# ScalarE multiplies and shifts x itself in a transformer layer's prologue, and first-feature products and transposes are reordered

## The chip, the cores and the metric

The kernel runs on one core of a Trainium2 chip. A core has five engines with instruction queues of their own: TensorE (PE in the profile; its weight loads are PEld) for matrix products and transposes, VectorE (DVE), ScalarE (ACT), GpSimd (POOL), and SyncE (SP), which here issues the transfers from DRAM. Operands lie in SBUF, products collect in PSUM. Semaphores order the engines among each other, and every engine works off its own queue in order.

The metric is the device time of one execution in microseconds, compared by the median over runs.

## The reference

One layer of a diffusion backbone works on 128 context tokens and 512 latent tokens, 1024 features wide. Only its first steps matter here: a normalisation, a modulation by conditioning vectors (one pair of scale and shift per feature for the context tokens, another for the latent tokens), and the product with the input weights, of which the prologue takes the key and value columns.

```python
ada_ctx = (jax.nn.silu(c_ctx) @ w_ada[i] + b_ada[i])[None, None, :]
ada_lat = (jax.nn.silu(c) @ w_ada[i] + b_ada[i])[:, None, :]
...
sh1, sc1, g1, sh2, sc2, g2 = jnp.split(ada, N_ADA, axis=-1)
u = rms_norm(h, p["g_pre1"]) * (1 + sc1) + sh1
z = u @ p["w_in"]
q, k, v, b_gate, c_gate, x_in, g_att, g_conv = jnp.split(z, idx, axis=-1)
```

Behind that stand attention, a gated convolution, the output projections and a convolutional feed-forward part. They make up most of the time, and the change does not touch them.

## The kernel before

Inputs are float32. A float32 product is made of three products of split operands: each operand is divided into a high part, rounded to the type `fp32r`, and a low part, the remainder. `mm3` (lines 182 to 185) adds high by high (L183), high by low weights (L184) and low by high weights (L185). The roundings are ScalarE copies, the remainders VectorE subtractions.

The 640 tokens are five tiles of 128 (tile 0 is context), the 1024 features eight blocks of 128, called features below: the first is number 0. The prologue goes so:

- The five token tiles are loaded into `XT`, squared on ScalarE (L351), normalised on VectorE into `xn` (L356), transposed by TensorE (`x_turn`, L361: eight 128x128 transposes for one tile) into PSUM, and copied to `xT` with features on the partitions (`x_copy`, L367 on ScalarE and L369 on VectorE).
- For each feature scale and shift are computed from `w_ada`. The features go in groups: (0), (1), (2, 3), (4, 5), (6), (7). `ada1_mm(g, i)` (L379) multiplies the conditioning vectors with the group's columns, i = 0 for scale and 1 for shift; each call is eight matmuls. `ada1_copy` (L386) brings the sums to SBUF as `e`, by ScalarE. `ada1_fold` (L393) sums partial results by a product with `sel`, and two VectorE instructions for each feature (L396, L398) write its columns of `scsh`: scale and shift for latent and context tokens. `ada1_fold(2, (0,))` does feature 2, `ada1_fold(2, (1,))` feature 3 alone.
- `modulate(f, a, b)` (L403 to L416) makes the operand of feature f for tokens a to b. VectorE writes `u`, x times scale plus shift, in one instruction for context tokens and one for latent tokens (L411). ScalarE rounds it into the high part `UH` (L413). VectorE subtracts for the low part `UL` (L416).
- `fetch` and `cut_upto` load the weight units of `w_in` (`raw`) and split them, `whi` by ScalarE (L148) and `wlo` by VectorE (L149); the first unit is split by lines of its own (L476, L478).
- `kv_mm(f, ts)` (L418) adds feature f's three products for the token tiles ts into the PSUM sums of keys and values, all 512 columns at once.

The order of TensorE, ScalarE and VectorE is written out by hand, and each runs its instructions in just the order of the code; SyncE's too in the prologue. What is written first is first in the queue, and an instruction that waits holds up all behind it on its engine. The lines around the first three features:

```python
        ada1_mm(1, 0)
        kv_mm(0, (0, 1))
        modulate(0, 512, NTOK)
        cut_upto(2)
        ada1_mm(1, 1)
        ...
        kv_mm(0, (2,))
        ada1_fold(1)
        kv_mm(0, (3, 4))
        modulate(1, 0, 384)
        modulate(1, 384, NTOK)
        ada1_mm(2, 0)
        ada1_copy(2, 0, 1)
        kv_mm(1, (0, 1))
```

From feature 2 on a loop does the same for each feature: ada products where a group is due, the split of the next unit, `kv_mm` for tiles 0 and 1, fold and `modulate` of the next feature, `kv_mm` for tiles 2 to 4.

`XT` is used again: once normalised, its rows take columns of `w_ada` for later groups. The region of `xT` for features 4 to 7 is used again as `AR`, for a later stage's columns of `w_ada`, loaded at L229 and used at L235.

Of the kernel before, what the change touches and what calls it, by code (L numbers as in the profile page):

```python
# [13 lines left out]
AF = mybir.ActivationFunctionType  # L14
ALU = mybir.AluOpType
# [3 lines left out]
KT = 8  # L19
# [44 lines left out]
def trunk_layer(ctx, tc, x_prompt, x_sample, cache_k, cache_v, c, c_ctx, w_ada, b_ada, g_pre1, g_post1, g_pre2,  # L64
# [3 lines left out]
    V, S, G, PE = nc.vector, nc.scalar, nc.gpsimd, nc.tensor  # L68
# [25 lines left out]
    def nm(s):  # L94
        cnt[0] += 1
        return f"{s}_{cnt[0]}"

    def region(pool, tag, shape, dtype, name):
        return pool.tile([128] + shape, dtype, tag=tag, name=name)
# [16 lines left out]
    def ps2():  # L116
        return ps.tile([128, 1024], F32, tag="s2", name=nm("s2"), bufs=3)

    def ps1():
        return psa.tile([128, 512], F32, tag="s1", name=nm("s1"), bufs=2)  # L120
# [7 lines left out]
    state = {"next": 0, "raw": [], "cut": [], "limit": 10}  # L128
# [25 lines left out]
    def fetch(i):  # L154
        while len(state["raw"]) < min(i, len(units), state["limit"]):
            w, k0, nk, c0, n = units[len(state["raw"])]
            if nk * n > 512:
                raw = raw_tile()
            else:

                if not halves:
                    raw = raw_tile()
                    halves.extend([raw[:, 512:1024], raw[:, 0:512]])
                raw = halves.pop()
            nc.sync.dma_start(raw[:, :nk * n].rearrange("p (k c) -> p k c", c=n),
                              w[k0 * 128:(k0 + nk) * 128, c0:c0 + n].rearrange("(k p) c -> p k c", p=128))
            state["raw"].append(raw)
# [14 lines left out]
    def mm3(out, ah, al, bh, bl, start, stop):  # L182
        PE.matmul(out, ah, bh, start=start, stop=False)  # L183
        PE.matmul(out, ah, bl, start=False, stop=False)  # L184
        PE.matmul(out, al, bh, start=False, stop=stop)  # L185
# [26 lines left out]
    scsh = const.tile([128, KT, 4], F32, name="scsh")  # L212
# [5 lines left out]
    UH = region(ra, "r0", [KT, NTOK], F32R, "UH")  # L218
    UL = region(ra, "r1", [KT, NTOK], F32R, "UL")
# [71 lines left out]
    with tc.tile_pool(name="pro", bufs=2) as pro, tc.manual_schedule(engines={mybir.EngineType.SP}):  # L291
# [21 lines left out]
        def araw_tile():  # L313
            return pro.tile([128, 1024], F32, tag="araw", name=nm("araw"), bufs=4)

        def ada_loads(g, rooms):
            n, c = len(GROUPS[g]), GROUPS[g][0] * 128
            araws[g] = rooms
            for i, raw in enumerate(rooms):
                o, k = (D, 0)[i // n], i % n * (KT // n)  # L320
                nc.sync.dma_start(raw.rearrange("p (k c) -> p k c", c=128 * n),
                                  w_ada[k * 128:(k + KT // n) * 128, o + c:o + c + 128 * n].rearrange("(k p) c -> p k c", p=128))
# [22 lines left out]
        xT = Halves(NTOK, F32, "xT")  # L345
        xns, rs, xps, pas, es = {}, {}, {}, {}, {}
# [8 lines left out]
            xns[t] = pro.tile([128, D], F32, tag="xn", name=nm("xn"), bufs=XB)  # L355
            V.tensor_scalar(out=xns[t], in0=XT[:, t, :], scalar1=rs[t], scalar2=None, op0=ALU.mult)  # L356

        def x_turn(t):
            p = xps[t] = ps2()
            for k in range(KT):  # L360
                PE.transpose(p[:, k * 128:(k + 1) * 128], xns[t][:, k * 128:(k + 1) * 128], ident)  # L361

        def x_copy(t, hf):
            src = xps[t].rearrange("p (k c) -> p k c", c=128)[:, 4 * hf:4 * hf + 4]
            dst = xT.half(hf)[:, :, t * 128:(t + 1) * 128]
            if t > 0 and hf == 0:
                S.activation(dst, src, AF.Copy)  # L367
            else:
                V.tensor_copy(dst, src)  # L369

        def ada1_mm(g, i):

            n = len(GROUPS[g])
            if i == 0:
                pas[g] = ps1()
            out = pas[g][:, i * 128 * n:(i + 1) * 128 * n]
            for k in range(KT):
                j, raw, m = 32 * (k % 4), araws[g][i * n + k * n // KT], k % (KT // n) * 128 * n
                PE.matmul(out[j:j + 32, :], s32[:, 32 * k + 30:32 * k + 62], raw[:, m:m + 128 * n], start=k < 4, stop=k >= 4,  # L379
                          tile_position=(0, j))  # L380

        def ada1_copy(g, a=0, b=2):
            n = len(GROUPS[g])
            if a == 0:
                es[g] = pro.tile([128, 512], F32, tag="e", name=nm("e"))
            S.activation(es[g][:, a * 128 * n:b * 128 * n], pas[g][:, a * 128 * n:b * 128 * n], AF.Copy)  # L386

        def ada1_fold(g, which=(0, 1)):

            n, pa = len(GROUPS[g]), pas[g]  # L390
            which = [i for i in which if i < n]
            for i in sorted(i + j for i in which for j in (0, n)):
                PE.matmul(pa[:, 2 * i:2 * i + 2], es[g][:, i * 128:(i + 1) * 128], sel[:, 0:2], start=True, stop=True)  # L393
            for i in which:
                f = GROUPS[g][i]
                V.tensor_scalar(out=scsh[:, f, 0:2], in0=pa[:, 2 * i:2 * i + 2], scalar1=feat[:, F_B + 8 + f:F_B + 9 + f],  # L396
                                scalar2=feat[:, F_PRE1 + f:F_PRE1 + 1 + f], op0=ALU.add, op1=ALU.mult)
                V.tensor_scalar(out=scsh[:, f, 2:4], in0=pa[:, 2 * (n + i):2 * (n + i) + 2], scalar1=feat[:, F_B + f:F_B + 1 + f],  # L398
                                scalar2=None, op0=ALU.add)
# [2 lines left out]

        def modulate(f, a=0, b=NTOK, between=()):  # L403

            if a == 0:
                us[f] = pro.tile([128, NTOK], F32, tag="u", name=nm("u"))
            u = us[f]
            for i, (s0, s1) in ((1, SEGS[0]), (0, SEGS[1])):
                c, d = max(a, s0), min(b, s1)
                if c < d:  # L410
                    V.tensor_scalar(out=u[:, c:d], in0=xT.at(f)[:, c:d], scalar1=scsh[:, f, i:i + 1], scalar2=scsh[:, f, 2 + i:3 + i],  # L411
                                    op0=ALU.mult, op1=ALU.add)
            S.activation(UH[:, f, a:b], u[:, a:b], AF.Copy)  # L413
            for x in between:
                x()
            V.tensor_tensor(out=UL[:, f, a:b], in0=u[:, a:b], in1=UH[:, f, a:b].bitcast(F32), op=ALU.subtract)  # L416

        def kv_mm(f, ts):  # L418
            for t in ts:
                sl = slice(t * 128, (t + 1) * 128)  # L420
                mm3(kvp[t], UH[:, f, sl], UL[:, f, sl], *state["cut"][f].at(0), f == 0, f == KT - 1)
# [22 lines left out]
        normal(0)  # L444
        square(2)
        x_turn(0)
        normal(1)
        square(3)
# [19 lines left out]
        x_copy(3, 0)  # L468
        ada1_copy(0)
        x_copy(3, 1)  # L470
        ada1_fold(0)
        x_turn(4)

        whi, wlo = (wp.tile([128, 1024], F32R, tag=x, name=nm(x), bufs=3)[:, 0:512] for x in ("whi", "wlo"))
        raw = state["raw"][0][:, 0:512]
# [6 lines left out]
        kvp = [kv01[:, 0:512], kv01[:, 512:1024], kv23[:, 0:512], kv23[:, 512:1024], kv4a[:, 0:512]]  # L482
# [4 lines left out]
            ada1_copy(g)  # L487


        ada1_mm(1, 0)  # L490
        kv_mm(0, (0, 1))
        modulate(0, 512, NTOK)
        cut_upto(2)
        ada1_mm(1, 1)
# [1 line left out]
        ckrt = araw_tile()  # L496
        fetch(5)
        ada_loads(3, [XT[:, 4, :]] + [araw_tile() for _ in range(3)])
        kv_mm(0, (2,))
        ada1_fold(1)  # L500
        kv_mm(0, (3, 4))
        modulate(1, 0, 384)
        modulate(1, 384, NTOK)
        ada1_mm(2, 0)
        ada1_copy(2, 0, 1)
        kv_mm(1, (0, 1))
        ada1_mm(2, 1)
        cut_upto(3)
        ada1_copy(2, 1, 2)
        fetch(6)  # L510
        kv_mm(1, (2,))
        ada1_fold(2, (0,))
        kv_mm(1, (3, 4))
        modulate(2, 0, 384)
        modulate(2, 384, NTOK)
        ada1_fold(2, (1,))
        for f in range(2, KT):
# [42 lines left out]
            if f == KT - 2:  # L560
                cut_upto(9)
                p = ps1()
# [7 lines left out]
                                op0=ALU.mult)  # L570
# [8 lines left out]
    with tc.tile_pool(name="att", bufs=2) as at:  # L579
# [313 lines left out]
        p = ps2()[:, 0:512]  # L893
# [42 lines left out]
        for g in range(NKV):  # L936
            if g and g + 1 < NKV:
                q_begin(g + 1)
            for i in range(0 if g else 1, 9):
# [16 lines left out]
                start, second, third_step = (g == 0 and i == n for n in (1, 2, 3))  # L956
# [139 lines left out]
    cut, raws, pair, TT = {}, {}, {}, {}  # L1096
# [12 lines left out]
    def block(out, key, half, right, start, stop):  # L1109
        _, hi, lo = cut[key]  # L1110
        wh, wl = (y[:, half * 512:half * 512 + 512] for y in (hi, lo))
        th, tl = TT[right]
        for k in range(4):
            ws = slice(k * 128, (k + 1) * 128)
            for n, (p, q) in enumerate(((wh, th), (wh, tl), (wl, th))):
                PE.matmul(out, p[:, ws], q[:, k, :], start=start and k == 0 and n == 0, stop=stop and k == 3 and n == 2,  # L1116
                          skip_group_check=True)
# [460 lines left out]
    def product(j, x):  # L1578
        b = 1 if x in ("A12", "S1", "S4") else 0
        part, half = PLACE[x]  # L1580
        block(pair[j][b], (j, part), half, RIGHT[x], x in ("A11", "A12", "S1"), True)
# [186 lines left out]
    for q in range(4):  # L1768
# [22 lines left out]
        for t in range(NT):  # L1791
            if q == 0:
                PA[t] = bank(t)
            for k in (2 * q, 2 * q + 1):
                sl = slice(t * 128, (t + 1) * 128)
# [193 lines left out]
    w, x, y = NJ - 3, NJ - 2, NJ - 1  # L1989
# [83 lines left out]
```

## Time and profile before

| | us |
|---|---|
| median of 3 runs | 1122.14 |
| fastest and slowest of them | 1122.09, 1122.76 |
| the profiled execution | 1123.04 |
| its span in the trace | 1121.3 |
| TensorE busy in the span | 1107.5 |
| VectorE, ScalarE, GpSimd busy | 795.6, 571.0, 149.2 |

Below, the rows of a timeline begin with the start and the duration in microseconds from the span's start; then come engine, line, operation, output and inputs, the shapes, how many instructions are taken together, and in brackets the idle time of the engine before and what ended it. A row of groups gives line, engine, operation, tiles, shapes and count; then the busy time in microseconds, the mean of one in nanoseconds, and the idle time ahead of them with what ended most of it. The chain of waits follows the work that ended last back from the last instruction and gives each engine's share of the span. An ordinary pass over float32 operands appears as more than one instruction in some rows (a product of two columns with `sel` counts twice, an ada call of eight matmuls sixteen times).

### The profile page before, as it was taken

Reading aid. Unit: us, or ns where it says so; the run is one execution under the profiler, and the core shown is the slowest. Engines: PE = TensorE matmul, PEld = TensorE weight load, DVE = VectorE, ACT = ScalarE, POOL = GpSimd, SP = SyncE. Lnnn points to the kernel's source line nnn. Section 1 sums busy time; section 2 is a strip of 40 time slices with the busy share of each in tenths; the row PEclk is TensorE's granted clock in tenths of the full one; section 3 lists DMA queues with packets and bytes.
Section 4 is the critical chain, followed back from the end, with each engine's and each line's share of the span. In section 5 each row is a group of like instructions: output and inputs, shape, how many; then the busy total and the mean of one; then the engine's idle time right before and its main releaser. Section 6 shows DMA issues by size and latency. Waiting matters only on the chain.

```text
span 1121.3 us, 19592 instructions
## 1 busy us (share of the span) xinstructions
PE 1107.5 (99%) x7885; PEld 1017.4 (91%) x7885; DVE 795.6 (71%) x1300; ACT 571.0 (51%) x1007; POOL 149.2 (13%) x191
## 2 busy tenths in 40 slices
PE   7999999999999999999999999999999999999997
PEld 5788888888999999999999889999999999998786
DVE  5687667654656798889645447888888888889544
ACT  5376766665235454544532247555655455556431
POOL 1056566652000000000000012000000000000001
PEclk9999999999999999999999999999999999999999
DMA  9744232423222223323332644233333233315722
GB/s 323 227 126 131 78 95 76 131 79 114 77 76 76 75 76 98 92 75 88 102 95 76 222 142 152 74 117 96 113 111 95 92 111 107 118 62 177 263 92 94
DMA packets 177304, 129.58 MB, mean 116 GB/s; under 512 B 6274, under 2 KB 159422, under 8 KB 177214
## 3 DMA queue, kind: packets, MB, share of 16 engines
q1 hardware_dynamic: 177102, 128.30, 37.1%
q8 instruction: 62, 1.02, 0.4%
q14 instruction: 28, 0.23, 0.1%
q10 hardware_dynamic: 112, 0.04, 0.0%
HBM read 116.87 MB, written 11.45 MB: 114 GB/s over the span
## 4 chain that ended last, share of the span: by engine, by line
PE 94%; DMA 2%; DVE 2%; ACT 1%; issue 0%; POOL 0%; DVEq 0%; POOLq 0%; SPq 0%; ACTq 0%
PE b L1116 44%; PE b L185 9%; PE b L183 9%; PE b L184 9%; PE s L659 3%; PE s L862 3%; PE s L838 3%; PE s L183 3%; PE s L185 3%; PE s L184 3%; PE s L235 1%; DMA raw<-in_w_in_dram 1%; DMA araw<-in_w_ada_dram 1%; PE b L1653 1%; PE s L630 0%; DMA XT<-in_x_sample_dram 0%
## 5 line engine op out<-in xcount | busy, mean ns | idle before, releaser
L1116 PE MATMUL b<-ZB,whi 128*128 128x320 f32 x1024 | 226.1, 309 | 0.0
L1116 PEld LDWEIGHTS b<-ZB,whi 128*128 128x128 f32 x1024 | 171.9, 188 | 1.8
L1116 PE MATMUL b<-ZB,wlo 128*128 128x320 f32 x512 | 158.1, 309 | 0.0
L1116 PE MATMUL b<-MT,whi 128*128 128x320 f32 x608 | 134.2, 309 | 0.0
L1116 PEld LDWEIGHTS b<-MT,whi 128*128 128x128 f32 x608 | 101.6, 188 | 0.0
L1116 PEld LDWEIGHTS b<-ZB,wlo 128*128 128x128 f32 x512 | 96.1, 188 | 0.3 <-DVE wlo L1107 0.3
L1116 PE MATMUL b<-MT,wlo 128*128 128x320 f32 x304 | 94.1, 309 | 0.1
L825 POOL TENSOR_TENSOR pr<-pr,sm 128x640 f32<-128x640 f32 x64 | 79.6, 1254 | 59.9 <-DVE sm L824 59.8
L1103 ACT ACTIVATE whi<-SUM 128x1024 fp32r<-128x1024 f32 x40 | 42.2, 1056 | 77.9 <-DVE SUM L1568 75.3
L1598 DVE SCALAR_TENSOR_TENSOR Y<-C,cffn,Y 128x642 f32<-128x642 f32 x88 | 77.7, 883 | 0.9
L815 ACT ACTIVATE pr<-s,mx,rq 128x640 f32<-128x640 f32 x64 | 56.6, 885 | 36.4 <-DVE mx L802 34.5
L1116 PE MATMUL b<-UL,whi 128*128 128x320 f32 x228 | 70.8, 311 | 0.0
L149 DVE TENSOR_TENSOR wlo<-raw,whi 128x1024 fp32r<-128x1024 f32 (+1 forms) x32 | 35.4, 1106 | 49.5 <-ACT whi L148 47.0
L1116 PE MATMUL b<-UH,wlo 128*128 128x320 f32 x228 | 70.0, 307 | 0.0
L1116 PE MATMUL b<-UH,whi 128*128 128x320 f32 x228 | 69.4, 304 | 0.0
L1103 ACT ACTIVATE whi<-WB 128x1024 fp32r<-128x1024 f32 x38 | 40.1, 1054 | 56.3 <-DVE WB L1211 56.3
L1107 DVE TENSOR_TENSOR wlo<-raw,whi 128x1024 fp32r<-128x1024 f32 (+1 forms) x51 | 50.4, 1019 | 25.3 <-ACT whi L1103 24.4
L183 PE MATMUL s<-whi,UH 128*128 128x256 f32 (+1 forms) x200 | 65.2, 326 | 0.6 <-ACT UH L413 0.5
L800 DVE TENSOR_REDUCE mx<-s 128x1 f32<-128x640 f32 x64 | 52.5, 820 | 16.7 <-PE s L659 15.9
L185 PE MATMUL s<-whi,UL 128*128 128x256 f32 (+1 forms) x200 | 61.3, 307 | 0.1
L1124 ACT ACTIVATE p<-b 128x320 f32<-128x320 f32 x78 | 34.1, 438 | 53.5 <-PE b L1116 51.9
L184 PE MATMUL s<-wlo,UH 128*128 128x256 f32 (+1 forms) x200 | 60.7, 304 | 0.0
(338 smaller groups left out, 2924.5 us busy)
## 6 DMA issues: line engine op xcount, KB each, us to landing
raw<-in_w_in_dram SPq DMA_DIRECT2D x48, 512.0 KB, 3.8
RAW<-in_w_up_dram SPq DMA_DIRECT2D x40, 512.0 KB, 3.8
raw<-in_w_ada_dram SPq DMA_DIRECT2D x30, 512.0 KB, 4.8
raw<-in_w_down_dram SPq DMA_DIRECT2D x22, 512.0 KB, 5.2
actd<-Y SPq DMA_DIRECT2D x18, 321.0 KB, 2.4
XT<-in_w_ada_dram SPq DMA_DIRECT2D x9, 512.0 KB, 6.9
raw<-in_w_conv_out_dram SPq DMA_DIRECT2D x9, 512.0 KB, 4.1
raw<-in_w_att_out_dram SPq DMA_DIRECT2D x8, 512.0 KB, 4.0
```

The costliest lines, as they stand in the source:

```text
L149: V.tensor_tensor(out=lo[:, :n], in0=raw, in1=hi[:, :n].bitcast(F32), op=ALU.subtract)
L183: PE.matmul(out, ah, bh, start=start, stop=False)
L184: PE.matmul(out, ah, bl, start=False, stop=False)
L185: PE.matmul(out, al, bh, start=False, stop=stop)
L800: V.tensor_reduce(out=mx, in_=self.sc[h], axis=AX.X, op=ALU.max, negate=True)
L815: S.activation(pr, self.sc[h], AF.Exp, bias=mx, scale=rs, accum_out=sm)
L825: G.tensor_tensor(out=pr, in0=pr, in1=sm.broadcast_to((128, NTOK)), op=ALU.mult)
L1103: S.activation(to[0], raw, AF.Copy)
L1107: V.tensor_tensor(out=lo, in0=raw, in1=hi.bitcast(F32), op=ALU.subtract)
L1116: PE.matmul(out, p[:, ws], q[:, k, :], start=start and k == 0 and n == 0, stop=stop and k == 3 and n == 2, skip_group_check=True)
L1124: S.activation(t, pair[j][b], AF.Copy)
L1598: V.scalar_tensor_tensor(out=y, in0=crows(j)[i][:, d:d + NACT], scalar=cffn[:, 44 * d + o:44 * d + o + 1], in1=y, op0=ALU.mult, op1=ALU.add)
```

## The change

`modulate` lets ScalarE write `UH` from `xT` itself, by the function Identity with the scale column as scale and the shift column as bias. It has one instruction for context tokens and one for latent tokens, as VectorE has. VectorE still writes `u` for the low part. The subtraction now waits for both.

`x_turn` can do part of a tile's transposes, and tile 4 is transposed in two halves around the first fold. `kv_first` does three token tiles of feature 0 in another order: all high by high, then, after an ada product, high by low weights and low by high weights. `kv_mm` calls of features 0 and 1 are divided differently among the ada products and folds, and `kv_mm(1, (0, 1))` comes ahead of `ada1_mm(2, 0)`.

```diff
-        def x_turn(t):
-            p = xps[t] = ps2()
-            for k in range(KT):
+        def x_turn(t, ks=range(KT)):
+            if ks[0] == 0:
+                xps[t] = ps2()
+            p = xps[t]
+            for k in ks:
                 PE.transpose(p[:, k * 128:(k + 1) * 128], xns[t][:, k * 128:(k + 1) * 128], ident)
...
                 if c < d:
-                    V.tensor_scalar(out=u[:, c:d], in0=xT.at(f)[:, c:d], scalar1=scsh[:, f, i:i + 1], scalar2=scsh[:, f, 2 + i:3 + i],
-                                    op0=ALU.mult, op1=ALU.add)
-            S.activation(UH[:, f, a:b], u[:, a:b], AF.Copy)
+                    x, sc, sh = xT.at(f)[:, c:d], scsh[:, f, i:i + 1], scsh[:, f, 2 + i:3 + i]
+                    S.activation(UH[:, f, c:d], x, AF.Identity, scale=sc, bias=sh)
+                    V.tensor_scalar(out=u[:, c:d], in0=x, scalar1=sc, scalar2=sh, op0=ALU.mult, op1=ALU.add)
             for x in between:
                 x()
             V.tensor_tensor(out=UL[:, f, a:b], in0=u[:, a:b], in1=UH[:, f, a:b].bitcast(F32), op=ALU.subtract)
 
+        def kv_first(ts):
+
+            (wh, wl), n = state["cut"][0].at(0), KT - 1
+            sls = [slice(t * 128, (t + 1) * 128) for t in ts]
+
+            def product(x, w, start):
+                for t, sl in zip(ts, sls):
+                    PE.matmul(kvp[t], x[:, 0, sl], w, start=start, stop=False)
+            product(UH, wh, True)
+            yield
+            product(UH, wl, False)
+            product(UL, wh, False)
+            yield
...
         x_copy(3, 1)
+        x_turn(4, range(4))
         ada1_fold(0)
-        x_turn(4)
+        x_turn(4, range(4, KT))
...
+        parts = kv_first((0, 1, 2))
+        next(parts)
         ada1_mm(1, 0)
-        kv_mm(0, (0, 1))
+        next(parts)
         modulate(0, 512, NTOK)
         cut_upto(2)
         ada1_mm(1, 1)
...
-        kv_mm(0, (2,))
+        kv_mm(0, (3,))
         ada1_fold(1)
-        kv_mm(0, (3, 4))
+        kv_mm(0, (4,))
         modulate(1, 0, 384)
         modulate(1, 384, NTOK)
+        kv_mm(1, (0, 1))
         ada1_mm(2, 0)
         ada1_copy(2, 0, 1)
-        kv_mm(1, (0, 1))
+        kv_mm(1, (2,))
         ada1_mm(2, 1)
         cut_upto(3)
         ada1_copy(2, 1, 2)
         fetch(6)
-        kv_mm(1, (2,))
+        kv_mm(1, (3,))
         ada1_fold(2, (0,))
-        kv_mm(1, (3, 4))
+        kv_mm(1, (4,))
         modulate(2, 0, 384)
         modulate(2, 384, NTOK)
         ada1_fold(2, (1,))
```

## The prediction

> **What bounds the kernel now.** I read the head of the page first, then its chain of waits.
>
> ```profile
> span 1121.3 us, 19592 instructions
> ...
> PE 94%; DMA 2%; DVE 2%; ACT 1%; issue 0%; POOL 0%; DVEq 0%; POOLq 0%; SPq 0%; ACTq 0%
> ```
>
> TensorE carries 94% of the chain that ends last. So a change to the prologue is worth what it takes from, or adds to, TensorE's waits there, and can be worth no more. All edits act within the prologue; behind it every engine has the same instructions in the same order. Next I read the groups by line (ScalarE alone, first 60 us), then the timelines of three engines through that stretch.
>
> ```profile
> L413 ACT ACTIVATE UH<-u 128x640 fp32r<-128x640 f32 (+4 forms) x11 | 6.5, 592 | 19.2 <-DVE u L411 19.2
> ```
>
> ScalarE idles 19.2 us ahead of its eleven roundings of `u`, always for VectorE's `u`. That is the wait the change goes for. Most of it costs nothing: TensorE has other products meanwhile. Where TensorE does wait shows in its rows.
>
> ```profile
> 17.82 0.50 PE L183 MATMUL s<-whi,UH 128*128 128x512 f32 x1 [0.49 <-ACT UH L413]
> ...
> 19.12 0.40 PE L184 MATMUL s<-wlo,UH 128*128 128x512 f32 x1
> 19.35 0.39 PE L185 MATMUL s<-whi,UL 128*128 128x512 f32 x1
> 19.67 0.65 PE L379 MATMUL s<-araw,s 128*32 128x128 f32 x16
> 20.25 0.50 PE L183 MATMUL s<-whi,UH 128*128 128x512 f32 x1
> ...
> 21.05 0.50 PE L393 MATMUL s<-sel,e 128*128 128x2 f32 x4
> 21.41 0.48 PE L183 MATMUL s<-whi,UH 128*128 128x512 f32 x1
> ...
> 22.98 1.07 PE L379 MATMUL s<-XT,s 128*32 128x256 f32 x16
> 23.98 0.50 PE L183 MATMUL s<-whi,UH 128*128 128x512 f32 x1
> ...
> 27.66 0.61 PE L393 MATMUL s<-sel,e 128*128 128x2 f32 x4
> 28.13 0.48 PE L183 MATMUL s<-whi,UH 128*128 128x512 f32 x1
> ...
> 30.70 0.50 PE L185 MATMUL s<-whi,UL 128*128 128x512 f32 x1
> ...
> 40.03 0.40 PE L185 MATMUL s<-whi,UL 128*128 128x512 f32 x1
> 40.53 0.50 PE L183 MATMUL s<-whi,UH 128*128 128x512 f32 x1
> ...
> 41.39 0.50 PE L185 MATMUL s<-whi,UL 128*128 128x512 f32 x1
> 41.73 0.39 PE L183 MATMUL s<-whi,UH 128*128 128x512 f32 x1
> ...
> 56.08 0.50 PE L185 MATMUL s<-whi,UL 128*128 128x512 f32 x1
> 56.42 0.39 PE L183 MATMUL s<-whi,UH 128*128 128x512 f32 x1
> ```
>
> Matmuls overlap, so a product's price is the distance between starts: 0.23 (19.12 to 19.35), and 0.34 for one that comes after a wait or another kind of work (41.39 to 41.73). A changeover to the ada products takes 0.32 (19.35 to 19.67). A 128-wide ada product (eight matmuls, in sixteen passes) then takes 0.58 (to 20.25), a 256-wide one 1.00 (22.98 to 23.98). A fold of two matmuls takes 0.36 (21.05 to 21.41), or 0.47 when it had to wait (27.66 to 28.13). A product follows ScalarE's or VectorE's last part by 0.05.
>
> **The change, part by part.** The other engines' rows:
>
> ```profile
> 16.12 0.21 DVE L398 TENSOR_SCALAR scsh<-s,feat 128x2 f32<-128x2 f32 x1
> ...
> 21.86 0.21 DVE L398 TENSOR_SCALAR scsh<-s,feat 128x2 f32<-128x2 f32 x1
> ...
> 23.37 0.56 DVE L416 TENSOR_TENSOR UL<-u,UH 128x384 fp32r<-128x384 f32 x1 [0.59 <-ACT UH L413]
> ...
> 28.58 0.21 DVE L398 TENSOR_SCALAR scsh<-s,feat 128x2 f32<-128x2 f32 x1
> ...
> 38.47 0.21 DVE L398 TENSOR_SCALAR scsh<-s,feat 128x2 f32<-128x2 f32 x1
> ...
> 38.91 0.79 DVE L411 TENSOR_SCALAR u<-xTb,scsh 128x128 f32<-128x128 f32 x2
> 40.51 0.82 DVE L416 TENSOR_TENSOR UL<-u,UH 128x640 fp32r<-128x640 f32 x1 [0.81 <-ACT UH L413]
> ```
>
> ```profile
> 17.14 0.63 ACT L413 ACTIVATE UH<-u 128x512 fp32r<-128x512 f32 x1 [1.45 <-DVE u L411]
> ...
> 22.81 0.52 ACT L413 ACTIVATE UH<-u 128x384 fp32r<-128x384 f32 x1 [2.04 <-DVE u L411]
> ...
> 26.71 0.63 ACT L148 ACTIVATE whi<-raw 128x512 fp32r<-128x512 f32 x1 [1.74 <-DMA raw<-in_w_in_dram]
> 27.25 0.36 ACT L386 ACTIVATE e<-s 128x256 f32<-128x256 f32 x1
> ```
>
> ```profile
> L1513 ACT ACTIVATE UFb<-b,mod 128x128 f32<-128x128 f32 x10 | 4.0, 457 | 1.0 <-PE b L1504 1.0
> ...
> L1751 ACT ACTIVATE C<-b 128x128 f32<-128x128 f32 x20 | 5.2, 259 | 0.0
> ...
> L413 ACT ACTIVATE UH<-u 128x256 fp32r<-128x256 f32 x2 | 0.8, 419 | 1.9 <-DVE u L411 1.9
> ...
> L413 ACT ACTIVATE UH<-u 128x128 fp32r<-128x128 f32 x1 | 0.3, 311 | 1.1 <-DVE u L411 1.1
> ```
>
> *Price of the new form.* ScalarE's multiply-add with scale and shift as column pointers, from SBUF and rounded, is not in the trace. Bounds: no surcharge over the plain rounding (0.31, 0.42, 0.52, 0.63 for 128, 256, 384, 512 columns), or the 0.20 by which L1513, the same function reading PSUM, exceeds a plain copy of that shape (0.457 against 0.259). I take 0.19, near the row of the same function: 0.50, 0.61, 0.71, 0.82. Two in a row overlap by about 0.10 (26.71 + 0.63 is 27.34, and the next starts at 27.25). Eleven instructions become nineteen; the cover is the 19.2 us of idle.
>
> *First feature.* Scale and shift end at 16.33 (16.12 + 0.21). The first 128 columns end at 16.37 + 0.50 = 16.87, so the first high product starts at 16.92 instead of 17.82. The next two token blocks lie in the 384-column piece: 16.77 + 0.71 = 17.48, products at 17.53 and 17.87. Then the ada product (18.19 to 18.77), which used to fill this very wait, and six low products (0.34 + 4 x 0.23 to the last, at 20.03), then the second ada product at 20.35. That was 19.67: 0.68 later with three more products (0.69) done. The gain of the reordering is nothing. Splitting the fifth tile's transposes puts four into the wait for `e`; they were needed before 16.9 anyway and hide behind the same scale and shift.
>
> *Second feature.* The fold of group 1 moves from 21.05 to 21.73, scale and shift end at 22.07 + 0.68 = 22.75. The first columns are ready at 22.79 + 0.50 = 23.29, the next 256 at 23.19 + 0.61 = 23.80, the low part at 23.83 + 0.56 = 24.39. TensorE finishes fold and the three products left of the first feature at 21.73 + 0.36 + 0.78 (0.32, 0.23, 0.23) = 22.87. Before, the 256-wide ada product (22.98 to 23.98) stood here and covered the rest; the change puts `kv_mm(1, (0, 1))` ahead of it. So TensorE waits to 23.34 (0.47), starts two products, and waits again from 23.91 to 24.44 (0.53). Behind this wait stand group 2's ada products and so ScalarE's `e`, the fold, and SyncE's loads into the same `XT` rows, which have at most 2.6 us less room (the first ada product now ends at 26.56, not 23.98); what they bring is used only with the seventh feature, so nothing waits.
>
> *To the fold of group 2.* From 24.44: the low product 0.34, block 1 and changeover 0.78, ada 1.00, block 2 and changeover 0.89, ada 1.00, block 3 0.80: 29.25 instead of 27.66, +1.59. The third weight unit, which set 27.66 (landed for ScalarE at 26.71), is no longer late.
>
> *Third feature.* This fold does not wait, 0.11 quicker: scale and shift end at 28.79 + 1.59 - 0.11 = 30.27, the 384 columns at 30.31 + 0.50 + 0.61 - 0.10 = 31.32, the low part at 31.91, its product at 31.96 instead of 30.70: +1.26. Only three products instead of six stand behind the fold, so TensorE waits here about 0.5.
>
> *Fifth feature.* Before, TensorE would have gone on at 40.26; it started at 40.53, then 41.39, and 41.73 instead of 40.95: 0.78 lost. Here the shorter chain pays. ScalarE starts at 38.72 instead of behind the second pair of folds and `u`: 38.72 + 0.50 + 0.82 - 0.10 = 39.94, low part 39.98 + 0.82 = 40.80 instead of 41.33, 0.54 gained (0.13 of wait remains): +0.72.
>
> *Eighth feature.* 56.08 to 56.42 is 0.34, a product that had waited; VectorE by then is late by less than TensorE, so 0.11 is recovered: **+0.61**.
>
> *A second wait on L416* (VectorE's own `u`, besides ScalarE): no row; 0 to 0.04 at four places. I take 0, since `u` is ready first.
>
> *SyncE's loads into `AR`* now wait for ScalarE's last high part instead of `u`, by 1.22 - 0.79 = 0.43 later:
>
> ```profile
> 54.42 0.99 SPq L229 DMA_DIRECT2D AR<-in_w_ada_dram  x2
> ```
>
> ```profile
> 64.94 1.08 PE L235 MATMUL s<-raw,s 128*32 128x128 f32 x32
> ```
>
> There are 10.5 us between issue and use; without that room it would cost 0.43.
>
> **Sum.** The profiled execution took 1123.04 around its span of 1121.3; the median of the runs is 1122.14. Adding 0.61: span 1121.9, runs 1122.7.
>
> **Rivals.** *Cheap form*: without the surcharge, the path loses 0.38 at each of the first three features and the 0.13 left at the fifth: 0.61 - 1.27 = -0.66, 1121.5. For it: only a bound. Against: L1513.
>
> *The wait at the second feature is filled* (ScalarE's and VectorE's parts come a microsecond sooner than I say): 0.61 - 1.00 = -0.39, 1121.8. Against: its price is made of rows.
>
> *No recovery*: ScalarE's two pieces take as long as `u` and rounding did, and the waits of the fifth and eighth features stay: +1.26, 1123.4. For this to decide, the surcharge would have to be near 0.4. The Trainium skill, "ScalarE: Activation LUTs", section "Rules for kernel authors", says to put multiplies and adds on VectorE, not ScalarE; by it the sum would be this one. The rows agree that the pair is dearer on ScalarE (1.22 against 0.79), yet there it replaces the rounding as well.
>
> *Slower beyond the bound: the clock.* The first twenty transposes took 4.53, later ones half as long each:
>
> ```profile
> 1.63 4.53 PE L296 MATMUL s<-ident 128*128 128x128 f32 x20 [1.63 <-POOL ident masks.py:199]
> 7.72 1.09 PE L361 MATMUL s<-ident,xn 128*128 128x128 f32 x8 [1.56 <-DVE xn L356]
> ```
>
> If the new waits (0.47, 0.53, 0.5) put TensorE back to half speed for such a stretch, 2.3 us are lost: +2.9, 1125.0. It decides if one wait suffices. Against: behind the 1.56 wait the eight transposes run at full speed. The Trainium skill, "TensorE: Matmul & The Clock Gate", section "What's actually happening", puts the fall at about 3.4 us of idleness; no run here shows that figure.
>
> *The change reaches further*, faster by over 2.2 us: the waits it touches sum to less.
>
> **How the numbers follow.** Forecast 0.58, cheap form 0.12, filled wait 0.10, no recovery 0.14, clock 0.04, faster 0.02. What a measurement can tell from no change is 0.2%, 2.24 us: the first four lie within it, 0.94. The range 1121.2 to 1123.9 holds these four, each with some 0.3 for the spread of the runs (1122.09 to 1122.76).
>
> **What would show it.** Right: L428's first row near 16.9, a wait of ScalarE's and VectorE's making ahead of the second feature's products near 23 to 24.4, the fold of group 2 near 29.2, the gap ahead of the fifth feature's low product nearly closed. Wrong: that fold before 28.3, ScalarE's 128-column form far from 0.50, or doubled spacing of products.

## The result, and the profile after

| | before | after |
|---|---|---|
| median of 22 runs each, us | 1122.18 | 1123.78 |
| fastest and slowest | 1122.02, 1123.10 | 1122.64, 1125.95 |
| ratio, 95% interval | | 1.0015, 1.0009 to 1.0021 |
| the profiled execution, its span | 1123.04, 1121.3 | 1124.26, 1122.4 |

The change costs 1.6 us, 0.15%. The forecast had 0.6. The time lies within the forecast's range and is no change by its bound of 0.2%, but almost two thirds of the loss are not in its sum. The head of the page after, and its chain of waits by engine:

```profile
span 1122.4 us, 19609 instructions
...
PE 96%; DVE 1%; ACT 1%; DMA 0%; POOL 0%; issue 0%; DVEq 0%; POOLq 0%; SPq 0%; ACTq 0%
```

TensorE's share of the chain rose from 94% to 96%, and that of the transfers fell from 2% to nothing. Now TensorE's rows of the first features after (start, duration, then what is done, and the wait in brackets):

```profile
17.30 1.33 PE L428 MATMUL s<-whi,UH 128*128 128x512 f32 x3 [0.59 <-ACT UH L415]
...
22.10 0.50 PE L395 MATMUL s<-sel,e 128*128 128x2 f32 x4
...
23.00 0.40 PE L185 MATMUL s<-whi,UL 128*128 128x512 f32 x1
23.70 0.50 PE L183 MATMUL s<-whi,UH 128*128 128x512 f32 x1 [0.29 <-ACT UH L415]
24.03 0.40 PE L184 MATMUL s<-wlo,UH 128*128 128x512 f32 x1
24.78 0.50 PE L185 MATMUL s<-whi,UL 128*128 128x512 f32 x1 [0.35 <-DVE UL L419]
...
29.61 0.50 PE L395 MATMUL s<-sel,e 128*128 128x2 f32 x4
...
32.29 0.51 PE L185 MATMUL s<-whi,UL 128*128 128x512 f32 x1 [0.35 <-DVE UL L419]
...
41.60 0.40 PE L185 MATMUL s<-whi,UL 128*128 128x512 f32 x1
...
42.06 0.40 PE L184 MATMUL s<-wlo,UH 128*128 128x512 f32 x1
42.40 0.50 PE L185 MATMUL s<-whi,UL 128*128 128x512 f32 x1
```

This is the walk of the forecast, all of it about 0.36 late. The fold of group 1 was forecast at 21.73 and stands at 22.10, that of group 2 at 29.25 (29.61), the third feature's low product at 31.96 (32.29). The two new waits are there: 23.00 to 23.70 is 0.70 where 0.23 is usual, and 24.03 to 24.78 is 0.75, so 0.47 and 0.52 are lost (forecast 0.47 and 0.53). From the last product of the fourth feature to the first low product of the fifth it takes 0.80 (41.60 to 42.40), where it took 1.36 before (40.03 to 41.39): 0.56 is made good.

The 0.36 comes from ahead of the changed instructions. The ada products of group 0, which nothing in the change touches, start 0.46 late; before, then after, with the transposes ahead of them:

```profile
13.32 1.40 PE L379 MATMUL s<-araw,s 128*32 128x128 f32 x32
```

```profile
9.41 4.43 PE L363 MATMUL s<-ident,xn 128*128 128x128 f32 x24 [0.31 <-DVE xn L356]
13.78 1.33 PE L381 MATMUL s<-araw,s 128*32 128x128 f32 x32
```

Windows of five microseconds (length, busy time of each engine, then the granted TensorE clock as third figure from the end), two before, then two after:

```profile
5.00:10.00 5.00, 3.13 (x22) 2.54 (x21) 2.15 (x4) 4.21 (x7) 2.29 (x6) 1.00 1.04 381
10.00:15.00 5.00, 3.66 (x51) 2.51 (x49) 4.85 (x10) 3.27 (x10) 1.97 (x4) 1.00 1.18 310
```

```profile
5.00:10.00 5.00, 2.84 (x18) 2.31 (x17) 2.11 (x3) 4.38 (x7) 2.38 (x6) 0.93 1.02 372
10.00:15.00 5.00, 4.96 (x55) 4.36 (x53) 4.78 (x10) 3.18 (x9) 1.89 (x5) 0.73 1.17 315
```

After, the clock stood at half speed from 9.3 to 12.7 us. That is not the whole delay: the first tile's transposes began 0.22 late (7.94 instead of 7.72), ahead of the drop.

If the same rows of TensorE are laid side by side (start after less start before), after is 0.86 us late at 62 us, still 0.86 at 86 us, and then 1.75 at 92 us. That step of 0.89 is no part of the prologue. The view of TensorE's waits (what it waited for: us in total, times, longest) shows it; before, then after:

```profile
PE s L838 <- ACT pr L815: 0.5, 1, 0.5
```

```profile
PE s L859 <- ACT pr L836: 1.4, 1, 1.4
```

`pr` belongs to the softmax of the attention stage and is made by ScalarE. Ahead of it in ScalarE's queue stands the split of a weight unit. The queues of SyncE and ScalarE around it, before:

```profile
82.90 0.37 SPq L165 DMA_DIRECT2D raw<-in_w_in_dram  x1
...
86.47 1.06 ACT L763 ACTIVATE whi<-raw 128x1024 fp32r<-128x1024 f32 x1
```

and after:

```profile
83.77 0.37 SPq L165 DMA_DIRECT2D raw<-in_w_in_dram  x1
...
88.67 1.06 ACT L784 ACTIVATE whi<-raw 128x1024 fp32r<-128x1024 f32 x1 [1.23 <-DMA raw<-in_w_in_dram]
89.63 0.87 ACT L836 ACTIVATE pr<-s,mx,rq 128x640 f32<-128x640 f32 x1
```

Before, the unit was there in time. After, the load took 1.4 us longer, and ScalarE stood still for 1.23 us with `pr` behind it. The transfers between issue and landing, before:

```profile
q1 hardware_dynamic: 878, 0.70, 70.7%
...
raw<-in_w_in_dram SPq DMA_DIRECT2D x1, 512.0 KB, 3.5
```

and after (queue, packets, MB, share of the sixteen DMA engines; then the load with its time from issue to landing):

```profile
q1 hardware_dynamic: 1522, 1.03, 69.2%
q14 instruction: 2, 0.02, 2.0%
...
raw<-in_w_in_dram SPq DMA_DIRECT2D x1, 512.0 KB, 4.9
```

Two packets of an instruction queue fall into the load, at 85.73 and 87.65 us, and none before. The load's landing is reported in sixteen parts. Before, all came 3.21 to 3.48 us behind the issue; after, fifteen came by 3.58 and the sixteenth at 4.88. One part held the unit up.

### The profile page after: what moved, and what is told of

Its sections match the earlier page's. It is cut to its first block, busy times and chain, and to the rows that moved or that the text cites. A ratio compares the mean times of both kernels' runs of the same rounds, so it can differ in the third digit from the quotient of the medians.

```text
span 1122.4 us, 19609 instructions
## 1 busy us (share of the span) xinstructions
PE 1108.2 (99%) x7885; PEld 1019.1 (91%) x7885; DVE 795.3 (71%) x1300; ACT 575.7 (51%) x1015; POOL 149.3 (13%) x191
## 4 chain that ended last, share of the span: by engine, by line
PE 96%; DVE 1%; ACT 1%; DMA 0%; POOL 0%; issue 0%; DVEq 0%; POOLq 0%; SPq 0%; ACTq 0%
PE b L1137 45%; PE b L185 9%; PE b L183 9%; PE b L184 9%; PE s L680 3%; PE s L883 3%; PE s L859 3%; PE s L183 3%; PE s L185 3%; PE s L184 3%; PE s L235 1%; PE s L381 1%; PE b L1674 1%; DMA XT<-in_x_sample_dram 0%; PE s L651 0%; PE b L1525 0%
```

## The experiments

All runs of before beside them have medians of 1122.19, 1122.28 and 1122.26. "Offset" is the start of a row of TensorE less the start of the same row in the profile of before, which is itself an execution 0.86 us above its median. Three theories stood at the start. A: the forecast's sum, in which the second feature's order loses and the form gains. B: the form itself loses. C: what lies beyond the sum comes from the unit near 88 us.

### One half of the change at a time

`form_alone` is the kernel before with the new `modulate`:

```diff
-                    V.tensor_scalar(out=u[:, c:d], in0=xT.at(f)[:, c:d], scalar1=..., scalar2=..., op0=ALU.mult, op1=ALU.add)
-            S.activation(UH[:, f, a:b], u[:, a:b], AF.Copy)
+                    S.activation(UH[:, f, c:d], x, AF.Identity, scale=sc, bias=sh)
+                    V.tensor_scalar(out=u[:, c:d], in0=x, scalar1=sc, scalar2=sh, op0=ALU.mult, op1=ALU.add)
```

> The order of before, with ScalarE's multiply-add form. Theory A (the order of the second feature loses, the form gains): the fold of group 2 stays at 27.66 by the third weight unit, low product of the third feature 0.2 earlier, fifth feature's about 0.85 earlier, end of the prologue 1.0 earlier: about 1121.1. Theory B (the form itself loses): slower than before, by 0.5 or more. Theory C (the changed kernel's extra time beyond my sum lies behind the prologue, in a weight unit's landing near 88 us): the prologue gains, but the total does not move in step with it.

Measured: 1121.89 us, ratio 0.9996 (0.9987 to 1.0004). `order_alone` is the changed kernel with the old `modulate`, the same lines the other way round.

> The changed kernel's order, with before's u and rounding (the form undone). Theory A: the waits at the first two features grow: fold of group 1 at 22.3, fold of group 2 at 30.0, low product of the third feature at 32.9, nothing recovered at the fifth feature: prologue 2.2 later than before, about 1124.4. Theory B: back at or below before, 1122.2.

Measured: 1125.16 us, ratio 1.0029 (1.0020 to 1.0039). So the form does not lose, and B falls; the order does, by nearly 3 us with the old form and less with the new. The form gained less than the 1.1 us that A gives it, 0.3 by the medians. Its offset is -1.62 at 62 us and -1.03 at 92 us; but that is against a slow prologue. `before_plus8` below is the kernel before with eight idle ScalarE instructions more, and its offset is -0.24 at 7.7 us, -0.63 at 14 us and -0.84 at 62 us, and still -0.84 at 92 us. So the 0.86 by which the profiled execution of before is slow lies ahead of 62 us. Its fold of group 2, at 27.66 in that profile, stands in `before_plus8` at

```profile
26.85 0.61 PE L395 MATMUL s<-sel,e 128*128 128x2 f32 x4
```

### The second feature's order

`ada_first` is the changed kernel with the ada product back in its place:

```diff
-        kv_mm(1, (0, 1))
         ada1_mm(2, 0)
         ada1_copy(2, 0, 1)
+        kv_mm(1, (0, 1))
         kv_mm(1, (2,))
```

> The changed kernel with one move undone: group 2's first ada product and its copy again ahead of the second feature's products for tiles 0 and 1. Theory A: the product covers the two waits at 23 to 24.4, fold of group 2 at 28.05 instead of 29.25, prologue 0.7 earlier than before, about 1121.4. Theory B: stays slower than before by 0.6 or more. Theory C: prologue 1.2 shorter than the changed kernel's, total less regular.

Measured: 1122.15 us, ratio 1.0000 (0.9991 to 1.0008). `second_as_before` restores all calls of that feature:

```diff
-        kv_mm(1, (0, 1))
         ada1_mm(2, 0)
         ada1_copy(2, 0, 1)
-        kv_mm(1, (2,))
+        kv_mm(1, (0, 1))
...
-        kv_mm(1, (3,))
+        kv_mm(1, (2,))
         ada1_fold(2, (0,))
-        kv_mm(1, (4,))
+        kv_mm(1, (3, 4))
```

> The changed kernel with the second feature's products placed as before throughout (first feature as changed). Theory A: fold of group 2 back at 27.66, prologue 1.0 earlier than before, the same end as with the form alone, about 1121.1: what was done at the first feature is worth nothing either way. Theory B: slower than before. If the reordering of the first feature is of use, this is faster than the form alone by up to 0.7.

Measured: 1122.09 us, ratio 0.9997 (0.9988 to 1.0006). The two lie 1.63 and 1.69 us below the changed kernel, where the expectations are 1.3 and 1.6 below its forecast. Group 2's folds, from the timelines of TensorE in `order_alone`, `form_alone`, `ada_first` and `second_as_before`:

```profile
29.53 0.50 PE L395 MATMUL s<-sel,e 128*128 128x2 f32 x4
```

```profile
27.03 0.61 PE L393 MATMUL s<-sel,e 128*128 128x2 f32 x4
```

```profile
27.45 0.50 PE L395 MATMUL s<-sel,e 128*128 128x2 f32 x4
```

```profile
27.08 0.50 PE L395 MATMUL s<-sel,e 128*128 128x2 f32 x4
```

But all four lie 0.7 to 1.0 us above theory A. In the three with the new form the unit adds to that, as C says: between 86 and 92 us the offset steps up by 0.59 in `form_alone`, 0.50 in `ada_first` and 1.29 in `second_as_before`. But further back these three make good about 0.65 again, in two steps that are told below, so the unit leaves a net loss in `second_as_before` alone, of 0.6. In `order_alone` the offset doesn't step at the unit, so the late load goes with the form, not with the order. What is left above A, 0.8 in `order_alone` and about as much in `form_alone` and `ada_first`, lies ahead of 62 us by the offsets, and its cause stays open.

### Whose instructions are fetched

Theory D: ScalarE has eight instructions more, so its next block of instructions is fetched earlier, into the load. `before_plus8` adds eight to the kernel before, the other three sixteen, to push the packet out ahead of the load:

```diff
         rows1 = load_rows((c[0:1, :], c_ctx.unsqueeze(0), b_ada.unsqueeze(0), g_pre1), nc.scalar)
+        for _ in range(8):
+            S.activation(warm, mhalf[:, 0:1], AF.Silu)
```

> The kernel before, with eight 128x1 ACTIVATEs more on ScalarE at its start, where it waits for x (ScalarE is idle from 2.23 to 4.81 us there): nothing else is changed, and no result depends on them. Theory D: the new form's eight more ScalarE instructions move ScalarE's instruction fetch (8 KB packets on the instruction queue, at 87.5 and 89.9 us in the kernel before) forward in time into the load of a w_in unit (issued at 82.9 us, landed 3.48 us later in the kernel before), and one of the load's sixteen parts stands behind it. Then here, without the new form, the packets come at 84 to 86 us, fifteen parts land within 3.6 us of the issue and the last after 4.5 to 5.3 us, ScalarE's split of the unit waits 0.9 to 1.3 us, TensorE's rows are unchanged at 62 us and 0.6 to 1.2 later at 92 us, and the time is 1122.8 to 1123.4. Theory E: the landing depends on what the new form itself does (on ScalarE and the memory) or on the moment of the load's issue. Then the landing stays at 3.5 us, and the time at 1122.2.

Measured: 1122.58 us, ratio 1.0003 (0.9994 to 1.0012).

> The order of before with the new form, and sixteen 128x1 ACTIVATEs more on ScalarE at the start. Theory D: the instruction packets come some 5 us earlier than with the form alone (83.7 and 85.7 us there), ahead of the load's first bytes at about 82.3 us; the landing is 3.5 us again instead of 4.59, the 0.6 us that the unit gave back stays, and the time is 1121.3 (form_alone: 1121.9). Theory E: landing 4.6 us, 1121.9.

Measured: 1124.07 us, ratio 1.0017 (1.0008 to 1.0026).

> The changed kernel with the second feature's products as before, and sixteen 128x1 ACTIVATEs more at the start. Theory D: the landing falls from 5.29 to 3.5 us, the 1.29 us that the unit gave back stays, and the time is 1120.9 to 1121.2 (second_as_before: 1122.1), the fastest of all kernels here. Theory E: 5.3 us, 1122.1.

Measured: 1123.91 us, ratio 1.0015 (1.0007 to 1.0024).

> The changed kernel itself with sixteen 128x1 ACTIVATEs more at the start. Theory D: the landing falls from 4.88 to 3.5 us, the 0.9 us that the changed kernel lost between 83 and 92 us is gone, and the time is 1122.7 to 1123.0, which is what the forecast's sum gave. Theory E: 4.9 us, 1123.8.

Measured: 1125.72 us, ratio 1.0031 (1.0019 to 1.0042).

D falls in this form. In `before_plus8` the load landed in 3.47 us, and the packets stood where they had stood, against the load's issue. In the others the last part landed at 4.84 to 5.15. They are slower for another reason, which ScalarE's rows in `form_plus16` show:

```profile
2.78 3.72 ACT L309 ACTIVATE warm<-mhalf 128x1 f32<-128x1 f32 x16 [0.55 <-ACT warm L293]
6.41 1.04 ACT L353 ACTIVATE junk<-XT 128x1024 f32<-128x1024 f32 x1
```

Sixteen took 3.72 us, 0.23 each, more than the idle stretch that was to cover them; the first square came at 6.41 instead of 4.81, and all behind it later; their clock also stood at half speed for 3.4 us or more, from 9.5, 9.6 and 8.3 us on. So these three say nothing on the fetch's place ahead of the load.

What the traces so far do show is who fetches. The packet that meets the load, or in three kernels passes behind it, comes when VectorE has started 185 to 187 instructions, semaphore instructions counted, in all ten. ScalarE stood at 145 to 161 by then, depending on the kernel. The other packet is no rival: it comes when GpSimd has started 61 instructions in every kernel, 3.9 to 4.6 us behind the load's issue whether the load is late or not, and where the load is late the fifteen other parts are already down. VectorE's records tell why it comes sooner: up to 82 us they hold 25 semaphore instructions before and 36 after, and the eleven new ones all stand at the subtraction (L419), which now waits for two engines.

### VectorE's fetch moved

Theory D2: it is VectorE's. Twelve copies at its start, where it is idle for most of the first 6.9 us, move its fetch by twelve instructions:

```diff
         rows1 = load_rows((c[0:1, :], c_ctx.unsqueeze(0), b_ada.unsqueeze(0), g_pre1), nc.scalar)
+        tiny = pro.tile([128, 16], F32, name="tiny", bufs=1)
+        for i in range(12):
+            V.tensor_copy(tiny[:, i:i + 1], mhalf[:, 0:1])
```

> The kernel before with twelve 128x1 copies on VectorE at its start, where it waits for the first square (idle from 2.0 to 6.9 us); no result depends on them. Theory D2: the packet that holds up the w_in unit's load near 83 us is VectorE's instruction fetch, since it comes when VectorE has executed 185 or 186 instructions in every kernel so far (at 89.9 us in before, at 83.65 in form_alone, whose VectorE has some 14 instructions more by then). Then here it comes at 84 to 85.5 us, 1 to 2.5 us behind the load's issue; fifteen parts of the load land within 3.6 us and the last after 4.5 to 5.3 us; TensorE's rows lie 0.5 to 1.2 us later at 92 us than at 86 us, against the same rows of before; the time is 1122.7 to 1123.4. Theory E (the load is late for another reason that comes with the new form): landing 3.5 us, no step between 86 and 92 us, 1122.2.

Measured: 1122.68 us, ratio 1.0003 (0.9994 to 1.0012). ScalarE's split, the chain of waits and the transfers of this kernel:

```profile
87.26 1.06 ACT L766 ACTIVATE whi<-raw 128x1024 fp32r<-128x1024 f32 x1 [1.12 <-DMA raw<-in_w_in_dram]
```

```profile
82.47 4.77 DMA raw<-in_w_in_dram
```

```profile
q14 instruction: 2, 0.02, 2.2%
```

The old kernel, with the old form and the old order, now shows the same late load, and the chain that ends last goes through it.

> The order of before with the new form, and the same twelve copies. Theory D2: VectorE's packet comes at 78 to 80 us, ahead of the load's issue at 81.3 us; all sixteen parts land within 3.6 us, no step between 86 and 92 us, and the time is 1121.2 to 1121.4 (form_alone: 1121.9), faster than before. Theory E: landing 4.6 us, a step of 0.6 us, 1121.9.

Measured: 1120.90 us, ratio 0.9988 (0.9979 to 0.9997). The split and the transfers:

```profile
85.14 1.06 ACT L767 ACTIVATE whi<-raw 128x1024 fp32r<-128x1024 f32 x1
```

```profile
q1 hardware_dynamic: 893, 0.71, 62.7%
...
raw<-in_w_in_dram SPq DMA_DIRECT2D x1, 512.0 KB, 3.5
```

No wait, no instruction packet in the load.

> The changed kernel with the second feature's products as before, and the same twelve copies. Theory D2: packet ahead of the load, landing 3.5 us instead of 5.29, the step of 1.29 us between 86 and 92 us gone, and the time 1120.8 to 1121.2, the fastest here. Theory E: landing 5.3 us, 1122.1.

Measured: 1120.88 us, ratio 0.9988 (0.9979 to 0.9996).

> The changed kernel itself with the same twelve copies. Theory D2: landing 3.5 us instead of 4.88, the step of 0.84 us between 86 and 92 us gone, and the time 1122.7 to 1123.0, about the forecast's sum. Theory E: landing 4.9 us, 1123.8.

Measured: 1122.55 us, ratio 1.0002 (0.9994 to 1.0011). Group 2's fold and TensorE's wait for `pr` here:

```profile
28.59 0.50 PE L398 MATMUL s<-sel,e 128*128 128x2 f32 x4
```

```profile
PE s L862 <- ACT pr L839: 0.5, 1, 0.5
```

In all four the packet, the landing and the step came as D2 says, and E falls. Of the times `second_v12` lies within its range, and the three others at or below the lower end: 1122.68 for 1122.7, 1120.90 for 1121.2 and 1122.55 for 1122.7. The load in all kernels, from the landing events (the packet by the count of VectorE's started instructions):

| kernel | load issued | VectorE's packet (count) | 15th part, last part, after the issue | TensorE's wait for `pr` |
|---|---|---|---|---|
| before | 82.90 | 89.92 (185) | 3.47, 3.48 | 0.5 |
| before_plus8 | 82.06 | 89.05 (185) | 3.46, 3.47 | 0.5 |
| order_alone | 84.61 | 91.86 (185) | 3.43, 3.44 | 0.5 |
| before_v12 | 82.47 | 84.35 (187) | 3.46, 4.77 | 1.3 |
| form_alone | 81.28 | 83.65 (186) | 3.48, 4.59 | 1.1 |
| ada_first | 81.61 | 83.80 (186) | 3.54, 4.49 | 1.0 |
| second_as_before | 81.21 | 83.96 (187) | 3.44, 5.29 | 1.8 |
| after | 83.77 | 85.73 (186) | 3.58, 4.88 | 1.4 |
| form_plus16 | 82.67 | 84.58 (186) | 3.66, 4.88 | 1.4 |
| second_plus16 | 82.57 | 84.60 (186) | 3.52, 5.15 | 1.7 |
| after_plus16 | 85.54 | 87.54 (186) | 3.53, 4.84 | 1.4 |
| form_v12 | 81.58 | 78.26 (183) | 3.46, 3.50 | 0.5 |
| second_v12 | 81.48 | 78.15 (183) | 3.40, 3.45 | 0.5 |
| after_v12 | 82.99 | 79.66 (183) | 3.41, 3.46 | 0.5 |

Behind the load's issue by 7 us or ahead of it by 3, the packet does nothing; at 1.9 to 2.8 us behind the issue it makes one of sixteen parts 1.0 to 1.9 us late.

Two smaller steps go with the same shift of VectorE's stream. In the changed kernel TensorE makes good 0.38 us between 400 and 450 us and 0.28 between 900 and 940; `before_v12` and `form_v12` make good as much, `before_plus8` and `order_alone` 0.02 and nothing. What stood in the way there before was not followed.

## Why the prediction was right, and where its sum was short

- *Price of the form*: right. ScalarE's rows after for a pair (128 and 384 columns), for 128 columns alone, and for a triple (128, 256 and 256):

```profile
16.75 1.09 ACT L415 ACTIVATE UH<-xTa,scsh 128x128 fp32r<-128x128 f32 x2 [0.68 <-DVE scsh L400]
...
18.36 0.50 ACT L415 ACTIVATE UH<-xTa,scsh 128x128 fp32r<-128x128 f32 x1
...
23.15 1.48 ACT L415 ACTIVATE UH<-xTa,scsh 128x128 fp32r<-128x128 f32 x3 [1.33 <-DVE scsh L400]
```

  From the prices of the forecast, less 0.10 for each overlap, they are 1.11, 0.50 and 1.52. The cheap form is out. The Trainium skill, "ScalarE: Activation LUTs", section "What ACT_TABLE_LOAD costs", adds about 93 ns for each pointer operand; two make 0.19, and these rows agree (0.50 for 128 columns, where the plain rounding took 0.31).
- *First feature, no gain*: right. `second_v12` has its new order and `form_v12` its old one: 1120.88 and 1120.90.
- *Second feature*: right in place and size. The fold of group 2 stands 1.95 later than in the profile of before (29.61, 27.66), and without the 0.36 from ahead that is 1.59, the sum's own figure. The difference of `after_v12` and `second_v12`, which differ in this feature alone, is 1.67 us. The filled wait is out.
- *Recovery at the fifth feature*: right, 0.56 where 0.54 was forecast. The rival without recovery is out.
- *The whole prologue*: forecast +0.61. `after_v12` against `before_v12`, which share the twelve copies, is 0.53 late at 86 us; by the medians it is -0.13, and with the 0.78 added by which only `before_v12` steps up at the unit, +0.65.
- *A second wait on L416*: this step failed. It was priced at 0 to 0.04 us at its place, and at its place it costs nothing. But each of the eleven second waits is an instruction more in VectorE's queue, and these moved a fetch into a load. The other sentence that covered it, that behind the prologue every engine has the same instructions in the same order, is true of the instructions and not of when their blocks are fetched. The sum lacked +0.89 at the unit, and -0.38 and -0.28 further back, 0.23 in all. That is the smaller part of the 1.0 us that it lacks.
- *The clock*: the rival was that the new waits bring the half speed back. They did not. The drop in the profile after lies ahead of them, from 9.3 to 12.7 us. Another one lies from 8.8 to 12.3 us in `second_as_before`, at 1122.06 us. The forecast's argument against the rival, eight transposes at full speed behind a wait of 1.56, does not hold in every execution: in `form_alone` the same eight took 1.97 us instead of 1.09, behind a wait of 1.33.

The balance does not close. The steps behind the prologue come to 0.23 us, so by the medians 1.4 of the 1.6 us lie in the prologue, where the sum had 0.61. Between the two kernels with the copies the prologue costs 0.65, as forecast. Reckoned in the same way (median, less the steps of the kernel's own profile), the copies go with a prologue 0.3 longer in the old kernel and 0.4 shorter in the changed one, and why was not settled: the copies at VectorE's start were not separated from the moved fetch in this.

The clock in the first 13 us is a candidate for a part. It stood at half speed behind 8 us in the profiles of all seven kernels that have the new form and no copies, and of none of the other seven; `order_alone`, one of those, is as far above its sum all the same. And the ten runs of the changed kernel with a granted clock of 0.999 have a median of 1123.52, the twelve below that 1124.20, the two slowest the lowest clock, 0.996; so the clock goes with the spread of 3.3 us in that kernel (0.4 in `after_v12`), but even at 0.999 the kernel is 1.3 above before. That the change brings the half speed about is not shown: it lies ahead of the changed instructions. What the profiles do show is that the walk was made on a slow execution: row by row it fits, but against a prologue 0.84 us longer than that of `before_plus8`, which took 1122.25.

Of the change, the new form is worth having and the second feature's new order is not: with that order left as it was and the fetch moved away from the load, the kernel takes 1120.9 us, 1.4 us less than before and 2.9 less than the changed kernel. Of the 1.4, some 0.7 are the two steps further back, which go with VectorE's moved stream. With the copies in both, the form itself is worth 1.0: `form_v12` lies 1.78 below `before_v12`, and 0.78 of that is the unit; without the copies, `form_alone` gained 0.3 with its load late.

## What to carry to other kernels

An edit's price is not only where it stands: every added wait or instruction moves the engine's later instruction fetches, and where one falls into a load that ends on the critical path, a microsecond can come or go a long way behind the edit. So when a small change has an effect in a stage that it does not touch, look at which of a load's parts land late, and for instruction packets beside it. And a walk of rows stands on one execution: compare it with a second one before taking its waits for usual. A wait is best filled with the longest work that is ready: the order that took the wide ada product out of the second feature's wait cost 1.7 us.

## What the runs showed of the hardware

An instruction packet of 8 KB, itself recorded as 0.4 to 1.4 us long, made one part of a 512 KB load 1.0 to 1.9 us late, while the fifteen others were down within 3.7 us of the issue, as without it; in `second_as_before` the packet took 0.55 us and the part was 1.85 late, so the packet's own time does not account for all of it. The Trainium skill, "DMA: Bandwidth & Descriptors", section "Queues, rings and completion order", says that each DMA engine takes turns between its queues, a whole packet at a time; one late part of sixteen agrees with that, and the delay beyond the packet's time does not follow from it.
